# The S5 output factors move from two single buffers into the shared ring of six

## The chip, the cores and the metric

The kernel runs as one launch on one core of one Trainium2 chip. The metric is the device time of an execution in microseconds (us). Three executions were timed and one further execution was profiled. The engines are TensorE (PE, with its weight loads shown apart as PEld), VectorE (DVE), ScalarE (ACT), GpSimd (POOL) and SyncE (SP). SP does no arithmetic here: it issues every DMA of the program, in one order that is fixed when the program is built.

## The reference, cut to what matters

A single trunk layer works on 256 context tokens and 256 latent tokens of width 2048. One input projection feeds two mixers: RWKV-7 with 16 heads, and an S5 state space of 64 groups with 64 complex states each, in both directions. An output projection, a ConvGLU channel mixer and a final norm follow. The part that matters here is the S5 output:

```python
sr, si = _s5_scan(bu_re, bu_im, lam_re, lam_im, s0, d == 1)
...
s5_y.append(jnp.einsum('ghp,btgp->btgh', lp['s5_c_re'][d], sr)
            - jnp.einsum('ghp,btgp->btgh', lp['s5_c_im'][d], si))
```

The kernel cuts the scan into chunks of 8 tokens. For that it needs C times the powers 0 to 8 of lambda (a complex product, so a real and an imaginary part with two products each), and from these the 8-token Toeplitz matrices that carry inputs to outputs inside a chunk.

## The kernel before, in words

The program has four stretches. The first modulates the tokens. The second projects them: 256 KB weight tiles `raw` (line 210, two buffers) are split into a high and a low part on ACT (L213) and DVE (L214), and PE multiplies them (L430). Beside the projections run the preparation of the RWKV factors (`prepare`: L570 to L692), five blocks of the modulation, and two functions that turn S5 parameters into matrices: `s5_factors` (increments, L1319 to L1328, result `mbd` in DRAM) and then `s5_toeplitz` (outputs, L1181 to L1204, results `mcd` and `td` in DRAM). The third stretch is the recurrence: `chain` (L794 to L877) for RWKV and `s5` (L1337 to L1418). The channel mixer is the fourth.

`s5_toeplitz` works through 16 groups (two for each of the 8 passes of its outer loop), and a group has two blocks, the real and the imaginary part, so there are 32 blocks. For a group, SP loads 64 KB of C into a single buffer (L1170). For a block, DVE makes the first product `MCk` (L1181, 128x576) and POOL the second product `mck` (L1182); DVE combines them in `MCk` (L1184 for the real, L1187 for the imaginary part); four matmuls of PE read `MCk` (L1195), and SP stores it to `mcd` (L1199, 288 KB). After the second block ACT copies the bank out (`ks`, L1202, one buffer), SP stores it (`kd`, L1203), and after every second group SP copies `kd` to `td` in DRAM (L1204), which waits until both `kd` stores of the pass have landed.

Both `MCk` and `mck` have one buffer. So L1181 of a block waits until the store of the block before has landed, and L1182 waits until L1184 or L1187 of the block before has read `mck`.

Other work shares the queues there. POOL runs the forward substitutions of `solve` (L710 to L718: 31 steps of a product, L716, and a subtraction, L718). SP issues, when the projections have ended and their memory is free, a burst of loads for the scan: `U` (L1217), the first three `MB` (L1337) and `ul` (L1218). The loads of the chain come after the stores of the Toeplitz stage: `PT` (L794, L798) and `own` (L807). The chain's first matmuls are L831.

Pools are stacked. `pp`, the ring of six buffers, is closed when the RWKV preparation ends, and the space goes to `mw` (buffers of the later modulation's weights, `modw`, L374, 512 KB for each load), `yp` and the chain's pools. Every engine's order of instructions is set by a scheduler with a timeline of its own when the program is built; PE's order for L1195 is kept as written.

Of the kernel before, what the change touches and what calls it, by code (L numbers as in the profile page):

```python
# [10 lines left out]
F32 = mybir.dt.float32  # L11
# [144 lines left out]
class Body:  # L156
# [998 lines left out]
    def s5_toeplitz(self, pool):  # L1155


        nc, tc, V = self.nc, self.tc, self.nc.vector
        self.td = [tc.dram_tile([128, 8, 128], F32, name="td%d" % e) for e in range(8)]
        Bd = pool.tile([128, 4, 2, 2, 16], F32, name="s5Bd", bufs=1)  # L1160
        V.memset(Bd, 0.0)
        self.mcd = [tc.dram_tile([128, 2, 576], F32, name="mcd%d" % e) for e in range(16)]
        sh = [128, 4, 9, 16]
        for e in range(8):
            L, bb = self.s5_group(pool, e)
            kd = tc.dram_tile([128, 240], F32, name="kd%d" % e)
            for h in range(2):
                ee = 2 * e + h
                C = pool.tile([128, 4, 2, 16], F32, tag="C", name="C", bufs=1)
                nc.sync.dma_start(out=C, in_=self.A["s5c"][:, 2 * ee:2 * ee + 2].rearrange("p g d i h -> p (g d) i h"))  # L1170
                for par in range(2):
                    hr = slice(64 * par, 64 * par + 64)
                    nc.scalar.activation(out=Bd[hr, :, :, par], in_=bb[hr, 4 * h:4 * h + 4], func=AF.Copy)
                Lv = [L[:, :, i, 4 * h:4 * h + 4].rearrange("p t n -> p n t").unsqueeze(3).to_broadcast(sh)
                      for i in range(2)]
                Cv = [C[:, :, i].unsqueeze(2).to_broadcast(sh) for i in range(2)]
                ps = self.bank("d")
                for i in range(2):
                    MC = pool.tile(sh, F32, tag="MC", name="MCk", bufs=1)
                    t = pool.tile(sh, F32, tag="mt", name="mck", bufs=1)  # L1180
                    V.tensor_tensor(out=MC, in0=Cv[0], in1=Lv[i], op=ALU.mult)  # L1181
                    nc.gpsimd.tensor_tensor(out=t, in0=Cv[1], in1=Lv[1 - i], op=ALU.mult)  # L1182
                    if i == 0:
                        V.tensor_tensor(out=MC, in0=MC, in1=t, op=ALU.subtract)  # L1184
                    else:
                        fl = "p n t h -> p (n t h)"
                        V.scalar_tensor_tensor(out=MC.rearrange(fl), in0=MC.rearrange(fl), scalar=-1.0,  # L1187
                                               in1=t.rearrange(fl), op0=ALU.mult, op1=ALU.subtract)
                    with tc.manual_schedule(engines={mybir.EngineType.PE}):
                        for d in (1, 0):  # L1190
                            for g in range(2):
                                m = MC[:, 2 * g + d, 0:8]
                                m = m if d else m[:, ::-1]
                                o = 112 if d else 0
                                nc.tensor.matmul(ps[32 * g:32 * g + 32, o:o + 128],  # L1195
                                                 lhsT=Bd[:, 2 * g + d, i].rearrange("p a h -> p (a h)"), rhs=m,
                                                 start=(i == 0 and d == 1), stop=(i == 1 and d == 0),
                                                 skip_group_check=True)
                    nc.sync.dma_start(out=self.mcd[ee][:, i], in_=MC.rearrange("p n t h -> p (n t h)"))  # L1199
                    yield  # L1200
                ks = pool.tile([64, 240], F32, tag="ks", name="ks", bufs=1)
                nc.scalar.activation(out=ks, in_=ps[0:64, 0:240], func=AF.Copy)  # L1202
                nc.sync.dma_start(out=kd.rearrange("(h q) n -> q h n", q=8)[4 * h:4 * h + 4], in_=ks)  # L1203
            nc.sync.dma_start(out=self.td[e].rearrange("(s h) q n -> s (h q) n", s=8),  # L1204
                              in_=bass.AP(kd.tensor, kd.offset, [[16, 8], [240, 128], [1, 128]]))
# [165 lines left out]
    def s5_outputs(self, pool, half):  # L1371
# [4 lines left out]
        for e in range(8 * half, 8 * half + 8):  # L1376
            MC = pool.tile([128, 2, 4, 9, 16], F32, tag="MC", name="MC", bufs=3)
            nc.sync.dma_start(out=MC.rearrange("p i n t h -> p i (n t h)"), in_=self.mcd[e])
# [285 lines left out]
```

## Time and profile before

| what | value |
|---|---|
| median of three timed executions | 2175.01 us (2169.95 to 2193.74) |
| profiled execution | 2184.84 us, its span 2183.1 us |
| mean granted TensorE clock | 0.895 of full speed |
| PE busy | 1913.8 us (88%) |
| DVE busy | 1274.7 us (58%) |
| ACT busy | 897.1 us (41%) |
| POOL busy | 336.4 us (15%) |
| DMA | 433.80 MB, mean 199 GB/s |

The span runs from the first to the last instruction; 1.7 us of the execution lie outside it. Busy shares are averages over stretches with different limits. A time stamp in the rows below is counted from the start of the span.

### The profile page before, as it was taken

How to read it: one execution, taken by the hardware profiler on the slowest of the kernel's cores; microseconds unless marked ns; L12 is line 12 of the kernel's file. 1: busy time of each engine (PE TensorE's matmuls, PEld its weight loads, DVE VectorE, ACT ScalarE, POOL GpSimd, SP SyncE). 2: the span in 40 equal slices, each digit the busy share in tenths (PEclk: the TensorE clock that was granted, in tenths of full speed). 3: DMA queues.
4: the chain of work that ended last, by engine and by line, in shares of the span. 5: the costliest groups of instructions: out<-in, count | busy, mean ns of one | idle time of the engine just before them, and what ended most of it. 6: DMA issues, size and time to landing. Idle time of an engine off the chain costs nothing.

```text
span 2183.1 us, 35662 instructions
## 1 busy us (share of the span) xinstructions
PE 1913.8 (88%) x13704; PEld 1470.4 (67%) x13704; DVE 1274.7 (58%) x2400; ACT 897.1 (41%) x1617; POOL 336.4 (15%) x517
## 2 busy tenths in 40 slices
PE   4899998998989813369989999999999999999997
PEld 1557766666767712256655767788888888888886
DVE  7526766577878633276113587766666656655454
ACT  2234644444645502132113344454455545544442
POOL 0200043073183272252000100000000000000000
PEclk8899998999999855576678999999999999999998
DMA  8873566545445643476475785456666665566664
GB/s 322 307 265 97 170 221 227 184 138 181 140 137 176 207 171 113 145 247 227 155 232 196 270 316 181 155 193 220 224 222 215 217 231 178 190 180 185 187 186 141
DMA packets 181147, 433.80 MB, mean 199 GB/s; under 512 B 27248, under 2 KB 59376, under 8 KB 178160
## 3 DMA queue, kind: packets, MB, share of 16 engines
q1 hardware_dynamic: 180976, 431.52, 59.8%
q8 instruction: 108, 1.77, 0.3%
q14 instruction: 63, 0.52, 0.1%
HBM read 373.12 MB, written 62.52 MB: 200 GB/s over the span
## 4 chain that ended last, share of the span: by engine, by line
PE 58%; DMA 11%; DVE 9%; issue 2%; ACT 2%; POOL 2%; SPq 1%; DVEq 0%; ACTq 0%; POOLq 0%
PE ps_w L230 25%; PE ps_m L230 11%; PE ps_w L430 4%; DMA mcd<-MCk 3%; PE ps_d L379 3%; PE ps_c L841 2%; DMA raw<-wout_in 2%; PE ps_s L1404 1%; DMA MB<-mbd 1%; PE ps_s L230 1%; PE ps_g L663 1%; DMA kd<-ks 1%; DVE lo L214 1%; DMA modw<-modw_in 1%; DVE MCk L1181 1%
## 5 line engine op out<-in xcount | busy, mean ns | idle before, releaser
L220 DVE TENSOR_TENSOR lo<-raw,hi 128x1024 fp32r<-128x1024 f32 (+1 forms) x327 | 371.2, 1137 | 232.0 <-ACT hi L219 227.9
L219 ACT ACTIVATE hi<-raw 128x1024 fp32r<-128x1024 f32 (+1 forms) x327 | 322.6, 987 | 293.3 <-PE ps_w L230 202.4
L230 PE MATMUL ps_m<-h,hi 128*128 128x512 f32 x688 | 248.2, 399 | 2.0 <-ACT hi L219 2.0
L230 PE MATMUL ps_w<-h,hi 128*128 128x512 f32 x688 | 248.6, 400 | 0.8 <-DVE h L1516 0.8
L230 PE MATMUL ps_w<-hid,hi 128*128 128x512 f32 x704 | 247.6, 398 | 0.0
L230 PE MATMUL ps_w<-hid,lo 128*128 128x256 f32 x704 | 195.1, 281 | 0.0
L230 PE MATMUL ps_m<-h,lo 128*128 128x256 f32 x688 | 187.9, 283 | 1.1 <-DVE lo L220 1.1
L230 PE MATMUL ps_w<-h,lo 128*128 128x256 f32 x688 | 186.5, 281 | 0.3 <-DVE lo L220 0.3
L430 PE MATMUL ps_w<-hhi,lo 128*128 128x512 f32 (+2 forms) x448 | 173.1, 387 | 10.7 <-DVE lo L214 10.6
L430 PE MATMUL ps_w<-hhi,hi 128*128 128x512 f32 (+2 forms) x448 | 174.4, 389 | 8.4 <-ACT hi L213 8.4
L214 DVE TENSOR_TENSOR lo<-raw,hi 128x512 fp32r<-128x512 f32 (+1 forms) x144 | 110.7, 772 | 120.2 <-ACT hi L213 110.8
L430 PE MATMUL ps_w<-hlo,hi 128*128 128x512 f32 (+2 forms) x448 | 167.7, 374 | 0.0
L213 ACT ACTIVATE hi<-raw 128x512 fp32r<-128x512 f32 (+1 forms) x144 | 88.7, 619 | 170.0 <-DMA raw<-win_in 74.6
L230 PEld LDWEIGHTS ps_w<-h,hi 128*128 128x128 f32 x688 | 129.2, 188 | 41.2 <-ACT up L238 10.9
L230 PEld LDWEIGHTS ps_w<-hid,hi 128*128 128x128 f32 x704 | 131.3, 188 | 31.4
L230 PEld LDWEIGHTS ps_m<-h,hi 128*128 128x128 f32 x688 | 130.0, 189 | 30.2 <-ACT hi L219 2.8
L230 PEld LDWEIGHTS ps_m<-h,lo 128*128 128x128 f32 x688 | 130.6, 190 | 5.6 <-DVE lo L220 1.8
L230 PEld LDWEIGHTS ps_w<-hid,lo 128*128 128x128 f32 x704 | 133.0, 189 | 1.5
L230 PEld LDWEIGHTS ps_w<-h,lo 128*128 128x128 f32 x688 | 129.9, 189 | 3.6 <-DVE lo L220 0.7
L1195 PE MATMUL ps_d<-MCk,s5Bd 128*32 128x128 f32 x256 | 31.9, 394 | 107.9 <-DVE MCk L1187 70.6
L430 PEld LDWEIGHTS ps_w<-hhi,lo 128*128 128x128 f32 (+1 forms) x448 | 87.9, 196 | 45.6 <-DVE lo L214 21.9
L430 PEld LDWEIGHTS ps_w<-hhi,hi 128*128 128x128 f32 (+1 forms) x448 | 88.4, 197 | 37.4 <-ACT hi L213 15.6
(387 smaller groups left out, 3633.7 us busy)
## 6 DMA issues: line engine op xcount, KB each, us to landing
raw<-wup_in SPq DMA_DIRECT2D x176, 512.0 KB
modw<-modw_in SPq DMA_DIRECT2D x152, 512.0 KB
raw<-wdn_in SPq DMA_DIRECT2D x80, 512.0 KB
raw<-win_in SPq DMA_DIRECT2D x140, 256.0 KB
own<-own SPq DMA_DIRECT2D x32, 1024.0 KB
modw<-modw_in SPq DMA_DIRECT2D x80, 256.0 KB
own<-own SPq DMA_DIRECT2D x32, 640.0 KB
raw<-wout_in SPq DMA_DIRECT2D x38, 256.0 KB
```

The lines of the kernel that those rows point to most:

```text
L213: nc.scalar.activation(out=hi, in_=raw, func=AF.Copy)
L214: nc.vector.tensor_tensor(out=lo, in0=raw, in1=hi.bitcast(F32), op=ALU.subtract)
L219: nc.scalar.activation(out=hi, in_=src, func=AF.Copy)
L220: nc.vector.tensor_tensor(out=lo, in0=src, in1=hi.bitcast(F32), op=ALU.subtract)
L230: mm = self.nc.tensor.matmul(out, lhsT=a, rhs=b, start=(n == 0), stop=(n == last), skip_group_check=True)
L379: self.behind(nc.tensor.matmul(ps[32 * j:32 * j + 32, :], lhsT=self.silu[:, k], rhs=ws[j], start=(k < 4), stop=(k >= 12)))
L430: self.nc.tensor.matmul(out, lhsT=w[:, j], rhs=x[:, k, lo:T], start=(k == 4 * job["qs"][0] and n == 0), stop=(k == 4 * job["qs"][1] - 1 an ...
L663: mm = nc.tensor.matmul(pss[h][:, 128 * c:128 * c + w], lhsT=BK[hr, 4 * s + c], rhs=X[hr, c, x1:x1 + w], start=True, stop=True)
L841: nc.tensor.matmul(U[q:q + 64, i], lhsT=pt[q:q + 64, :, 8 * i + n], rhs=Ws[q:q + 64, i], start=True, stop=True)
L1181: V.tensor_tensor(out=MC, in0=Cv[0], in1=Lv[i], op=ALU.mult)
L1195: nc.tensor.matmul(ps[32 * g:32 * g + 32, o:o + 128], lhsT=Bd[:, 2 * g + d, i].rearrange("p a h -> p (a h)"), rhs=m, start=(i == 0 and d = ...
L1404: nc.tensor.matmul(outs[q], lhsT=X, rhs=m[:, ::-1] if d else m, start=False, stop=(d == 1 and i == 1))
```

## The change

The two tiles of a block no longer have one buffer each in the pool `tp`. They are taken from `pp`, whose six buffers were used until then by the early modulation and by `s5_factors`. Shapes, instructions and their number stay as they are. Two of the six buffers go to each block, so a buffer comes round again after three blocks. The first blocks follow the last tiles of `s5_factors` in that ring. `C`, `ks` and `s5Bd` keep one buffer each, and the bank `d` stays single.

```diff
@@ s5_toeplitz
                 ps = self.bank("d")
                 for i in range(2):
-                    MC = pool.tile(sh, F32, tag="MC", name="MCk", bufs=1)
-                    t = pool.tile(sh, F32, tag="mt", name="mck", bufs=1)
+                    MC, t = (self.pp.tile([128, 576], F32, tag="pp", name=name, bufs=6)
+                             .rearrange("p (n t h) -> p n t h", n=4, t=9) for name in ("MCk", "mck"))
                     V.tensor_tensor(out=MC, in0=Cv[0], in1=Lv[i], op=ALU.mult)
                     nc.gpsimd.tensor_tensor(out=t, in0=Cv[1], in1=Lv[1 - i], op=ALU.mult)
```

The scheduler lays out every engine anew for this. On PE, around the last matmuls of the input projection (L430 with 32x256), there stood before (L1195 counts four matmuls for a block; L732 and L743 belong to the second half of `solve`):

```order
L430 MATMUL ps_w<-hhi,lo 32x256
L1195 MATMUL ps_d<-MCk,s5Bd 32x128 x32
L732 MATMUL ps_m<-AU,L_6698 32x32 x32
L1195 MATMUL ps_d<-MCk,s5Bd 32x128 x4
L732 MATMUL ps_m<-AU,L_6698 32x32 x32
L1195 MATMUL ps_d<-MCk,s5Bd 32x128 x4
L743 MATMUL ps_m<-PT,FN 32x32 x32
L1195 MATMUL ps_d<-MCk,s5Bd 32x128 x4
L743 MATMUL ps_m<-PT,FN 32x32 x32
L1195 MATMUL ps_d<-MCk,s5Bd 32x128 x60
```

and there stands now:

```order
L430 MATMUL ps_w<-hhi,lo 32x256
L1195 MATMUL ps_d<-MCk,s5Bd 32x128 x72
L1345 MATMUL ps_s<-U_8125,MB 64x64 x32
L732 MATMUL ps_m<-AU,L_6698 32x32 x32
L1345 MATMUL ps_s<-U_8125,MB 64x64 x16
L732 MATMUL ps_m<-AU,L_6698 32x32 x32
```

Behind the last projection matmul there were 104 matmuls of L1195, which is 26 blocks; now there are 72, which is 18 blocks or 9 groups. Fourteen blocks instead of six stand between the projections.

On SP, where the first stores of the Toeplitz stage stand among the weight loads of the projection, there stood before:

```order
L1199 DMA mcd_4158<-MCk 128x576
L210 DMA raw<-win_in 128x512
L1328 DMA mbd_2534<-MB 128x512
L374 DMA modw<-modw_in 128x1024
L1228 DMA ud_7178<-u 128x8x64
L1231 DMA uld<-ul 128x256
L210 DMA raw<-win_in 128x512
L374 DMA modw<-modw_in 128x1024 x2
L1170 DMA C<-s5c_in 128x128
L210 DMA raw<-win_in 128x512
L1199 DMA mcd_4158<-MCk 128x576
L210 DMA raw<-win_in 128x512 x2
```

and there stands now:

```order
L1170 DMA C<-s5c_in 128x128
L1228 DMA ud_7178<-u 128x8x64
L1231 DMA uld<-ul 128x256
L1199 DMA mcd_4158<-MCk 128x576 x2
L210 DMA raw<-win_in 128x512
L1148 DMA Ls<-s5Led 128x144
L1170 DMA C<-s5c_in 128x128
L1199 DMA mcd_4159<-MCk 128x576
L210 DMA raw<-win_in 128x512
L1203 DMA kd_4178<-ks 4x16x240
L1199 DMA mcd_4159<-MCk 128x576
```

A weight load now follows one or two stores of `MCk`, where several weight loads followed one store before. The three loads of `modw` have left this place; two of them now stand just ahead of the last `td` copy and the chain's `PT` loads, and the third behind those.

On POOL, where the last `solve` begins (L710), the difference is this:

```order
 L1320 TENSOR_TENSOR mt<-bs,Ls 128x512 x5
-L1182 TENSOR_TENSOR mck<-C,Ls 128x576 x2
-L589 MEMSET sg 128x8
+L589 MEMSET sg 128x8
+L1182 TENSOR_TENSOR mck<-C,Ls 128x576 x8
+L589 MEMSET sg 128x8
+L1182 TENSOR_TENSOR mck<-C,Ls 128x576 x8
+L710 MEMSET TM 128x1024
 L1182 TENSOR_TENSOR mck<-C,Ls 128x576
-L589 MEMSET sg 128x8
-L1182 TENSOR_TENSOR mck<-C,Ls 128x576 x3
-L710 MEMSET TM 128x1024
```

Before, 6 of the 32 products of L1182 stood ahead of the last `solve`, 8 inside it and 18 behind it. Now 18 stand ahead of it and 14 inside it, in pairs: one pair after 7 instructions of `solve`, the next after 23 more, and the other five pairs with 3 to 6 between them.

## Rows read from the trace of the kernel before

**Rows 1.** Page, busy tenths of PE in 40 slices of 54.6 us

```profile
PE   4899998998989813369989999999999999999997
```

**Rows 2.** Busy time by stretch; the last three columns are clock, DMA share and GB/s

```profile
700.00:720.00 20.00, 20.00 (x106) 13.78 (x105) 15.63 (x25) 9.24 (x20) 2.97 (x5) 1.00 0.66 211
720.00:740.00 20.00, 16.85 (x133) 14.46 (x131) 14.89 (x28) 14.84 (x36) 2.75 (x2) 0.83 0.65 217
740.00:760.00 20.00, 19.72 (x348) 16.33 (x347) 9.37 (x17) 12.33 (x26) 7.54 (x12) 0.83 0.43 136
...
860.00:880.00 20.00, 4.22 (x32) 2.32 (x33) 6.61 (x8) 1.96 (x6) 4.77 (x5) 0.50 0.33 108
...
920.00:940.00 20.00, 13.87 (x231) 13.11 (x233) 1.82 (x4) 6.80 (x18) 0.00 (x0) 0.50 0.91 275
```

**Rows 3.** Waits from 690 to 990 us: total, times, longest

```profile
DVE MCk L1181 <- DMA mcd<-MCk: 94.0, 25, 13.7
POOL mck L1182 <- DMA C<-s5c_in: 84.0, 14, 14.5
...
POOL mck L1182 <- DVE MCk L1184: 30.8, 12, 9.3
```

**Rows 4.** Chain that ended last, 690 to 990 us: start, duration, what

```profile
712.62 6.58 DMA raw<-win_in
...
863.69 1.09 PE ps_d L1195 x8
...
868.52 5.58 DMA mcd<-MCk
...
875.87 2.10 DMA mcd<-MCk
...
879.90 2.07 DMA mcd<-MCk
...
883.77 1.09 PE ps_d L1195 x8
...
905.54 2.54 DMA kd<-ks
```

**Rows 5.** Timeline of one group: start, duration, engine, line, instruction, idle before

```profile
863.26 0.38 SPq L1170 DMA_DIRECT2D C<-s5c_in  x1
...
865.47 1.21 POOL L1182 TENSOR_TENSOR mck<-C,Ls 128x576 f32<-128x576 f32 x1 [4.38 <-DMA C<-s5c_in]
866.15 1.14 DVE L1181 TENSOR_TENSOR MCk<-C,Ls 128x576 f32<-128x576 f32 x1 [2.52 <-DMA mcd<-MCk]
867.40 0.76 DVE L1184 TENSOR_TENSOR MCk<-MCk,mck 128x576 f32<-128x576 f32 x1
...
882.09 0.76 DVE L1181 TENSOR_TENSOR MCk<-C,Ls 128x576 f32<-128x576 f32 x1 [2.22 <-DMA mcd<-MCk]
```

**Rows 6.** Timeline from 685 to 780 us, where the projections end

```profile
710.60 1.06 SPq L374 DMA_DIRECT2D modw<-modw_in  x2
...
759.44 0.28 PE L430 MATMUL ps_w<-hhi,lo 128*32 128x256 f32 x1
759.75 1.74 SPq L1217 DMA_DIRECT2D U<-ud  x4
...
767.46 0.81 SPq L1199 DMA_DIRECT2D mcd<-MCk  x1
...
776.44 1.04 DVE L1181 TENSOR_TENSOR MCk<-C,Ls 128x576 f32<-128x576 f32 x1 [13.66 <-DMA mcd<-MCk]
```

**Rows 7.** Groups of instructions from 690 to 990 us: the last `solve` on POOL

```profile
L718 POOL TENSOR_TENSOR TM<-TM,tmp 128x31 f32<-128x31 f32 (+15 forms) x31 | 19.8, 639 | 2.2
L716 POOL TENSOR_TENSOR tmp<-AU,TM 128x31 f32<-128x31 f32 (+15 forms) x31 | 18.4, 592 | 2.0
```

**Rows 8.** Timeline from 905 to 990 us, where the chain begins

```profile
909.04 1.46 SPq L794 DMA_DIRECT2D PT<-pt  x2
...
931.28 0.45 PE L831 MATMUL ps_c<-ZE,own 128*64 128x64 f32 x2 [2.04 <-ACT ZE L814]
```

## The prediction

> **What bounds the kernel now.** I read the busy slices first. PE fills nearly every slice of the page but one run of four in the middle, where it falls to 1 to 6 tenths [rows 1]. The windows say what kind of stretch that is: from 860 to 880 us PE works 4.22 of 20 us, DVE 6.61, POOL 4.77, the DMA engines are at a third, and the granted clock is 0.50, the level of 1.2 GHz [rows 2]. No engine is full, so it is a stretch of latency. The list of waits names what it waits for: DVE's L1181 stood 94.0 us behind the store of `MCk`, and POOL's L1182 stood 84.0 us behind the load of C and 30.8 us behind DVE's L1184 [rows 3]. The chain of waits gives the rhythm: from one `td` pass to the next it is 863.69 to 883.77, 20.08 us for two groups, 10.04 us a group, and in each pass 5.58 + 2.10 + 2.07 = 9.75 us of the chain are store waits of the kind that the single buffer makes [rows 4].
>
> The stretch that can shrink begins at the last projection matmul, which ends at 759.7, and it ends at the first `PT` load at 909.0 [rows 6, 8]. That is 149.3 us, and 26 of the 32 blocks lie in it. Everything behind it, the chain's first matmul at 931.28 to begin with [rows 8], hangs on loads that SP issues after the last `td` copy.
>
> **The change, part by part.** No instruction is added or removed. What goes is the wait for the landed store and the wait of L1182 for L1184. What is late next is a sum of terms.
>
> *Term 1, eight blocks move into the projections.* PE's order has 18 blocks behind the last projection matmul in place of 26. The eight cost PE 8 x 1.09 / 2 = 4.4 us [rows 4], against 3.4 us that PE is idle from 700 to 760 [rows 2]. They cost DVE 8 x (0.76 + 0.76) = 12.2 us [rows 5], against 20.1 us of DVE idle there [rows 2]. If that cover held, the projections would end as now, at 759.7. SP is why it may not hold: a weight load now stands right behind one or two stores of `MCk`, which wait for a group's whole computation, and the weight tile has only two buffers. Were each of the seven groups there to take the 10.04 us of the present rhythm, with as much again for the last weight tile, the projections would run from 700 to 780. The three `modw` loads leave this place, which helps: a weight load issued behind two of them took 6.58 us [rows 4, 6]. Neither bound is nearer; I take 10 us of delay, an end at 770, and keep 760 and 780.
>
> *Term 2, up to the last six groups.* Three of the nine groups left run beside the burst of `U`, `MB` and `ul` loads, which remains: from its first issue to the landing of the store behind it are 759.75 to 776.44, 16.7 us [rows 6]. Beside it POOL has a pair of L1182 and then 23 instructions of `solve`, at (19.8 + 18.4) / 62 + 0.07 = 0.69 us each [rows 7], so 15.9 us, plus the pair of 2.4 us [rows 5]: 18.3 us. The two overlap. I take 19 us, and keep 16.7 and 24 us (a group's time more, should they not).
>
> *Term 3, the rhythm of six groups.* C has still one buffer: a load is issued when both products of the group before are made and the real part's store has been issued. From a load's issue to L1182 are 2.21 us, then two L1181 beside POOL at 1.14 us each, then L1184 at 0.76 us [rows 5], and with the store's issue and the signals some 0.6 us more: 5.9 us. POOL on its side has two products of 1.21 us [rows 5] and 3 to 6 instructions of `solve` at 0.69 us: 5.4 us. I take 6 us, keep 5.4 us below and 7 us above (half of the 2.54 us of a `kd` landing [rows 4] added, as every second group's store stands behind a `td` copy). Five periods are 30 us. The last group then needs 2.4 us on POOL, 0.8 us on DVE, 1.09 us on PE, about 0.5 us on ACT, 2.54 us for `kd` and 0.7 us for `td` [rows 4, 5]: 8 us.
>
> *Term 4, the moved `modw` loads.* They are 3 x 512 KB, and they now compete with the loads of the chain, where DMA already stands at 0.91 and 275 GB/s [rows 2]. At that rate 1.5 MB take 5.7 us. I take 5 us; they cost nothing if the chain waits for something else.
>
> *Sum.* 770 + 19 + 30 + 8 + 5 = 832 in place of 909: a gain of 77 us. The profiled execution of 2184.84 us becomes 2107.8. It stands 9.8 us above the median shown; counted from the median it is 2098. I put the number between them, at 2103. The bounds: 759.7 + 16.7 + 27 + 8 = 811.4 is a gain of 98 us, 2077 from the median; 780 + 24 + 35 + 8 + 6 = 853 is a gain of 56 us, 2129 from the profiled execution.
>
> The rows speak against a part of the change at one point: a product L1181 takes 1.14 us beside an L1182 on POOL and 0.76 us without one, while L1182 has its 1.21 us either way [rows 5], and the change puts every pair of L1181 beside a pair of L1182. With the price of 0.76 us a period would be 0.7 us shorter and five of them 3.5 us, which gives 2104 in place of 2108. The Trainium skill (GPSIMD Engine Reference, section Specifications) has a rule for it: GpSimd's SBUF interfaces are shared with VectorE, and VectorE instructions with two SBUF inputs contend with it. By that rule the dearer price holds, and the trace agrees, with VectorE as the one that pays.
>
> **The rivals.**
> - *C's single buffer keeps the old rhythm.* Then the change does less than it says. For it: 84.0 us of POOL's waits are for C [rows 3]. Against it: C's load waited in turn for L1181 of the imaginary part, which waited for a store. The last six groups at 10.04 us would make 770 + 19 + 50 + 10 + 5 = 854, a gain of 55 us: 2130 from the profiled execution. Chance 0.10.
> - *The weight loads are held longer than I take.* Six blocks, three groups, fill the 60 us before 759.7 today, 20 us a group, since DVE, ACT and POOL have other work in order between them. At 15 us a group the projections end at 700 + 105 + 10 = 815, and the sum is 877: a gain of 32 us, 2153 from the profiled execution and 2143 from the median. Chance 0.12.
> - *The third stretch gives some back.* From the first `PT` load to the first L831 are 22.2 us today [rows 8]. If the moved loads and a less lucky order doubled that, the gain is 77 - 22 = 55 us, 2130. Chance 0.08.
> - *Slower: SP's order ties the projections to the Toeplitz stage at today's pace.* The place is the weight load behind the stores of `MCk`; the price is seven times a group's time. At 20 us a group the projections end at 850, the sum is 912, and nothing is gained. Each further us a group costs 7 us, so from 23 us a group it is slower by over 1%; at 25 us it gives 947, that is 2223. Against it: of those 20 us, store waits and the waits of L1182 for L1184 are a part that the change removes. Chance 0.03 for slower and 0.05 for the ground around zero.
>
> **How the numbers follow.** The forecast has 0.62, with a range of its own of 2077 to 2129. The two cases at 2130 lie beside it, and the held weight loads reach from there to 2153. A range of 2077 to 2146 takes in the forecast, both cases at 2130 and about half of the held loads; outside are the rest of these (0.06), the ground around zero and the slower case (0.08) and a gain over 98 us (0.04): 0.18. About 1%, 22 us, is what a measurement of this kernel can tell from no change. Faster by more than that are the forecast, the old rhythm, the held loads and the third stretch: 0.92. Within it 0.05, slower 0.03.
>
> **What would show it.** In the profile of the changed kernel the wait of L1181 for `MCk`'s store should be gone. The last L430 should end at 760 to 780; later than that, and waiting for weights behind stores, it is the held loads. Behind it there should be about 60 us to the first `PT` load, with L1182 waiting for C for some 2 us a group and POOL busy with `solve` in between. A period near 10 us in the last six groups would show C's buffer as the new wait. The first L831 should follow the first `PT` load by 22 to 28 us. A shift of the third stretch that is smaller than the shift of the `PT` load would make term 4 wrong.

## The result, and the profile after the change

| | before | changed |
|---|---|---|
| median of the runs | 2182.14 us (4 runs, 2169.95 to 2193.74) | 2099.99 us (4 runs, 2091.06 to 2104.55) |
| profiled execution, span | 2183.1 us | 2099.2 us |

The ratio is 0.9619, with a 95% interval from 0.955 to 0.9688. The forecast was 2103 us, with a range of 2077 to 2146.

The page of the changed kernel answers to [rows 1]. The hole in the middle of PE's slices is smaller, and it is no longer a run of four slices at 1 to 6 tenths. The second row, the clock that PE was granted, becomes important further down.

```profile
PE   3899998998998872659989999999999999999997
...
PEclk9999998999979975676988999999999999999999
```

The waits from 690 to 990 us answer to [rows 3] (total, times, longest). L1181's 94.0 us behind `MCk`'s store have no row any more. L1182's wait for C is down from 84.0 to 16.6 us, its wait for L1184 from 30.8 to 2.2 us. What is new is that DVE's L1181 now waits for C as well.

```profile
DVE MCk L1181 <- DMA C<-s5c_in: 27.6, 8, 11.2
POOL mck L1182 <- DMA C<-s5c_in: 16.6, 7, 4.5
...
POOL mck L1182 <- DVE MCk L1184: 2.2, 1, 2.2
```

The timeline of PE and SP answers to [rows 6, 8] (start, duration, engine, line, instruction). The three rows are the end of the projections, the first `PT` load, and the first matmul of the chain.

```profile
775.33 0.28 PE L430 MATMUL ps_w<-hhi,lo 128*32 128x256 f32 x1
...
848.95 2.49 SPq L794 DMA_DIRECT2D PT<-pt  x1
...
880.04 0.37 PE L831 MATMUL ps_c<-ZE,own 128*64 128x64 f32 x1
```

**Where the 83.9 us of span went.** The first `PT` load moved from 909.0 to 848.9, which is 60.1 us. From there to the first L831 it is 31.1 us in place of 22.3, a loss of 8.8. From the first L831 to the first load of the output projection (`wout`), which I call the end of the third stretch, it is 296.0 us (880.0 to 1176.0) in place of 325.9 (931.3 to 1257.2), a gain of 29.9. All that follows is 2.7 us shorter. 60.1 - 8.8 + 29.9 + 2.7 = 83.9. So over 20 us were gained in a place that the change does not touch, where I had forecast a small loss.

The timeline of POOL shows the last groups. Each row is a pair of L1182, one group (start, duration, and in brackets the idle time before it).

```profile
778.70 3.48 POOL L1182 TENSOR_TENSOR mck<-C,Ls 128x576 f32<-128x576 f32 x2 [1.31 <-DMA C<-s5c_in]
...
798.87 2.38 POOL L1182 TENSOR_TENSOR mck<-C,Ls 128x576 f32<-128x576 f32 x2
...
804.55 3.50 POOL L1182 TENSOR_TENSOR mck<-C,Ls 128x576 f32<-128x576 f32 x2 [0.27 <-DMA C<-s5c_in]
...
814.90 3.48 POOL L1182 TENSOR_TENSOR mck<-C,Ls 128x576 f32<-128x576 f32 x2 [1.71 <-DMA C<-s5c_in]
...
838.99 3.47 POOL L1182 TENSOR_TENSOR mck<-C,Ls 128x576 f32<-128x576 f32 x2 [2.17 <-issue]
```

From 798.87 to 838.99 are five periods, 40.1 us, 8.0 us each in place of the old 10.04. The second thing to see is the duration: the pair at 798.87, beside whose first half DVE was waiting, takes 2.38 us, and the others take up to 3.50 us.

### The profile page after: what moved, and what is told of

The parts are those of the page before. It is cut to its first block, busy times and chain, and to the rows that moved or that the text cites. A ratio compares the mean times of both kernels' runs of the same rounds, so it can differ in the third digit from the quotient of the medians.

```text
span 2099.2 us, 35645 instructions
## 1 busy us (share of the span) xinstructions
PE 1872.6 (89%) x13704; PEld 1455.9 (69%) x13704; DVE 1295.6 (62%) x2400; ACT 898.2 (43%) x1617; POOL 347.9 (17%) x517
## 4 chain that ended last, share of the span: by engine, by line
PE 58%; DVE 10%; DMA 8%; POOL 4%; issue 3%; ACT 1%; SPq 0%; DVEq 0%; POOLq 0%; ACTq 0%
PE ps_w L230 27%; PE ps_m L230 12%; PE ps_w L430 4%; PE ps_d L379 2%; PE ps_c L841 1%; POOL TM L718 1%; PE ps_g L663 1%; POOL tmp L716 1%; DMA raw<-wout_in 1%; DMA modw<-modw_in 1%; PE ps_s L230 1%; PE ps_s L1345 1%; PE ps_s L1404 1%; DMA bs<-s5bbd 1%; DMA C<-s5c_in 1%
## 5 line engine op out<-in xcount | busy, mean ns | idle before, releaser
L430 PE MATMUL ps_w<-hhi,lo 128*128 128x512 f32 (+2 forms) x448 | 173.5, 388 | 15.5 <-DVE lo L214 15.4
L430 PE MATMUL ps_w<-hhi,hi 128*128 128x512 f32 (+2 forms) x448 | 174.6, 390 | 4.7 <-ACT hi L213 4.7
L430 PE MATMUL ps_w<-hlo,hi 128*128 128x512 f32 (+2 forms) x448 | 168.1, 375 | 0.0
L213 ACT ACTIVATE hi<-raw 128x512 fp32r<-128x512 f32 (+1 forms) x144 | 88.7, 619 | 170.2 <-DMA raw<-win_in 65.7
L430 PEld LDWEIGHTS ps_w<-hhi,lo 128*128 128x128 f32 (+1 forms) x448 | 88.3, 197 | 50.0 <-DVE lo L214 26.2
L430 PEld LDWEIGHTS ps_w<-hhi,hi 128*128 128x128 f32 (+1 forms) x448 | 89.0, 199 | 31.7 <-ACT hi L213 11.5
L430 PEld LDWEIGHTS ps_w<-hlo,hi 128*128 128x128 f32 (+1 forms) x448 | 88.8, 198 | 15.7 <-issue 2.9
```

Source lines behind the costliest of these rows:

```text
L213: nc.scalar.activation(out=hi, in_=raw, func=AF.Copy)
L430: self.nc.tensor.matmul(out, lhsT=w[:, j], rhs=x[:, k, lo:T], start=(k == 4 * job["qs"][0] and n == 0), stop=(k == 4 * job["qs"][1] - 1 an ...
```

## The experiments

The theory was that the store wait of L1181 was nearly the whole price, and that the third stretch is shorter because its granted clock is higher. Open were two rivals on the first point (both single buffers weigh alike; C's buffer is the next wait) and three on the second: the shorter gap ahead of the stretch sets the clock, the order of the work in it does, or it is chance. "Gap" is from the last L430 to the first `PT` load; "third" from that load to the first `wout` load; both from one profiled execution. Time and ratio are of all runs.

| kernel | last L430 | first PT | gap | third | clock in it | median us | ratio to before (95%) |
|---|---|---|---|---|---|---|---|
| before | 759.4 | 909.0 | 149.6 | 348.2 | 0.74 | 2182.14 | |
| changed | 775.3 | 848.9 | 73.6 | 327.1 | 0.80 | 2099.99 | 0.9619 (0.955 to 0.9688) |
| e2_store | 771.0 | 874.5 | 103.5 | 355.8 | 0.76 | 2139.84 | 0.9828 (0.9759 to 0.9897) |
| e3_mck | 763.2 | 908.3 | 145.1 | 325.0 | 0.82 | 2155.69 | 0.9884 (0.9824 to 0.9945) |
| e4_c2 | 781.2 | 849.7 | 68.5 | 348.0 | 0.78 | 2115.87 | 0.9699 (0.9636 to 0.9763) |
| e6_warm | 767.6 | 852.0 | 84.4 | 333.7 | 0.78 | 2115.03 | 0.9685 (0.9614 to 0.9757) |
| r1_before | 758.8 | 906.1 | 147.3 | 347.8 | 0.75 | 2178.31, one run | |
| r2_after | 772.6 | 849.4 | 76.8 | 318.7 | 0.83 | 2098.14 | 0.9624 (0.9588 to 0.966) |
| e7_dve | 771.3 | 849.1 | 77.8 | 358.5 | 0.76 | 2124.17 | 0.973 (0.9699 to 0.9761) |
| e8_dve_c2 | 777.5 | 843.2 | 65.7 | 298.6 | 0.87 | 2069.18 | 0.9493 (0.9464 to 0.9522) |
| e9_weave_after | 770.5 | 848.3 | 77.8 | 315.6 | 0.82 | 2084.63 | 0.9567 (0.9525 to 0.9608) |
| b_weave_before | 760.5 | 910.1 | 149.6 | 320.2 | 0.84 | 2152.27 | 0.9875 (0.983 to 0.9919) |
| e10_weave_dve_c2 | 777.8 | 843.2 | 65.4 | 305.1 | 0.83 | 2071.96 | 0.95 (0.944 to 0.9559) |

### One buffer at a time: e2_store and e3_mck

```
# e2_store, on the kernel before
-MC = pool.tile(sh, F32, tag="MC", name="MCk", bufs=1)
+MC = pool.tile(sh, F32, tag="MC", name="MCk", bufs=2)
# e3_mck, on the kernel before
-t = pool.tile(sh, F32, tag="mt", name="mck", bufs=1)
+t = pool.tile(sh, F32, tag="mt", name="mck", bufs=2)
```

> The kernel before with a second buffer for `MCk` alone, in the stage's own pool; `mck` stays single and the six early modulation buffers are not touched, so the three `modw` loads keep their early place. Theory (the store wait of L1181 was nearly the whole price): L1181's wait for `MCk`'s store is gone, a group is C's 2.2 us, two L1182 of 1.2 us with an L1184 and an L1187 of 0.77 us between and behind them, and 0.6 us of signals, about 6.8 us; 20 blocks in place of 26 lie behind the last projection matmul; 2100 to 2118 us. Rival (both single buffers weigh alike): L1182's wait for L1184 grows, the period stays at 8.5 to 9.5 us, 2130 to 2150 us. On the third stretch (first L831 to the first load of the output projection, 325.9 us before, 296.0 us with the change): if the granted clock behind a shorter gap sets it, it is between these two, nearer the shorter; if the moved `modw` loads and their order set it, it stays at 320 to 330 us.

> The kernel before with a second buffer for `mck` alone; `MCk` stays single. Theory (the store wait was nearly the whole price): L1181 still waits for the store, some 90 us over the stretch, 25 of 26 blocks stay behind the last projection matmul, the period falls by at most 1 us from 10.0 us; 2165 to 2182 us. Rival (both weigh alike): 2130 to 2150 us.

By the first `PT` load, e2_store has gained 34.5 us, e3_mck 0.7, and both together (the change) 60.1. So the two buffers do not add up: the second one of `mck` is worth nothing while the store wait stands. What the change has beyond e2_store is worth some 25 us more. That is the second buffer of `mck`, but also a third one of each tile, since the ring holds three blocks, and the `modw` loads that moved; these were not tried apart. The waits say why the single buffers do not add up, of e2_store first:

```profile
POOL mck L1182 <- DVE MCk L1184: 30.3, 11, 7.1
```

and of e3_mck:

```profile
DVE MCk L1181 <- DMA mcd<-MCk: 82.6, 26, 13.0
```

In e2_store the wait of L1182 for L1184 is as long as before [rows 3], and eight periods from 793.06 to 864.18 us average 8.9 us, not the 6.8 expected. The median of 2139.84 lies in the rival's range, and "nearly the whole price" is wrong: lifting the store wait alone gives 34.5 of 60.1.

The total of e3_mck surprised: 0.9884 of before, some 25 us and between the ranges of both accounts, with almost nothing gained by the first `PT` load. In the profiled execution 23.2 us of its gain are in the third stretch, 325.0 us in place of 348.2. That spoke against the gap as the cause, since this gap is as long as ever. In e2_store, whose gap is 46 us shorter, the stretch is longer than before (from the first L831 it is 336.0 us, over both expectations).

### Is it chance? r1_before and r2_after

Both kernels unchanged, traced once more.

> The kernel before, unchanged, for a second trace of it. Theory (each kernel's order in the third stretch sets its granted clock there and with it the stretch's length): from the first PT load to the first load of the output projection again 342 to 354 us (348.2 in the first trace), PE busy 295 to 308 us at a mean clock of 0.72 to 0.76. Rival (the clock of that stretch falls by chance from execution to execution, and the differences between kernels there are luck): anywhere from 325 to 356 us, as likely as not more than 8 us from 348.

> The changed kernel, unchanged, for a second trace of it. Theory (the order sets the third stretch): from the first PT load to the first load of the output projection 321 to 333 us (327.1 in the first trace), PE busy 265 to 278 us at a clock of 0.79 to 0.82, and 2090 to 2106 us in all. Rival (chance): 325 to 356 us, as likely as not more than 8 us from 327.

One row of each trace shows the third stretch (stretch, its length, busy time of PE, PEld, DVE, ACT and POOL, then clock, DMA share and GB/s). Before, first and second trace:

```profile
909.00:1257.20 348.20, 301.64 (x3419) 207.83 (x3417) 146.11 (x440) 85.27 (x198) 61.37 (x144) 0.74 0.67 223
```

```profile
906.10:1253.90 347.80, 300.95 (x3414) 208.76 (x3415) 145.57 (x440) 85.53 (x199) 62.56 (x144) 0.75 0.67 223
```

The changed kernel, first and second trace:

```profile
848.90:1176.00 327.10, 271.34 (x3684) 199.39 (x3685) 151.75 (x442) 92.69 (x206) 60.39 (x144) 0.80 0.74 247
```

```profile
849.40:1168.10 318.70, 264.51 (x3690) 194.99 (x3686) 150.50 (x441) 92.97 (x207) 60.40 (x144) 0.83 0.76 253
```

The kernel before repeats its 348 us within 0.4, its PE busy time within 0.7 and its clock within 0.01. The changed kernel repeats less closely, 8.4 us apart and 0.03 in the clock, beyond what I had expected, but both traces lie 20 to 30 us below before. Chance alone is out. And the difference is the clock: PE issues no fewer matmuls, 3684 and 3690 against 3419 (256 of the added ones are L732 and L743 of `solve`, which stand there now), yet is busy 30 to 37 us less. Of the same 512 matmuls of L841, one takes 299 ns in the second trace of before and 286 in that of the change (they overlap; together they keep PE busy for 57.7 and 46.8 us); of those of L379 that lie in the stretch, 868 against 679.

### Gap or order? e6_warm, b_weave_before and e9_weave_after

e6_warm keeps PE at work in the gap:

```
 with tc.manual_schedule(engines={mybir.EngineType.PE}):
+    for _ in range(3 if ee >= 10 else 0):
+        nc.tensor.matmul(ps[0:32, 256:512], lhsT=Bd[:, 0, 0].rearrange("p a h -> p (a h)"),
+                         rhs=Bd.rearrange("p n i a h -> p (n i a h)"), start=True, stop=True,
+                         skip_group_check=True)
     for d in (1, 0):
```

> The changed kernel with three added matmuls of 32x256 ahead of each pass of L1195 in the last six groups, 36 in all; they write columns of the bank that nothing reads. Nothing else is added. Theory (the granted clock behind the gap follows PE's idleness in it, and the third stretch gained by the clock): PE's busy share from 800 to 840 us rises from a quarter to over a half, the granted clock there leaves 0.50, the third stretch's mean rises from 0.83 to 0.88 or more and it falls from 296.0 us to 280 to 290 us; against that 0 to 8 us in the gap itself, where PE's passes get longer; 2085 to 2100 us. Rival (the third stretch gained by its order, and the clock follows its own load alone): clock and length of the third stretch stay as they are within 4 us, 2098 to 2110 us.

From 820 to 840 us the changed kernel and then e6_warm read:

```profile
820.00:840.00 20.00, 5.33 (x42) 2.94 (x40) 11.93 (x11) 2.94 (x9) 16.14 (x17) 0.50 0.45 147
```

```profile
820.00:840.00 20.00, 11.36 (x80) 6.44 (x76) 11.41 (x9) 1.96 (x6) 16.85 (x21) 0.91 0.50 157
...
860.00:880.00 20.00, 15.90 (x244) 13.69 (x246) 0.86 (x2) 10.25 (x21) 0.00 (x0) 0.50 1.00 285
```

The clock in the gap rose from 0.50 to 0.91 with PE's busy time, and it was back at 0.50, the level of 1.2 GHz, 20 us later. The third stretch did not follow: its clock was 0.78, and from the first L831 it was 313.7 us long, more than either account expected, as is the median of 2115.03 us. The clock raised in the gap was not carried into the stretch behind it. The order of PE's work there was laid anew too, though (3622 matmuls lie in the stretch, against 3684), so this run alone does not set the gap aside. The gap was 8 to 11 us longer, since the projections ended 5 to 8 us earlier and the first `PT` load came 3 us later, so nothing was won.

The other two edits leave all that lies ahead of the third stretch alone, and change one number that interleaves its two parts. The traces agree: up to the first `PT` load PE has the same 5160 matmuls in the same order in b_weave_before as before, and the same 4904 in e9_weave_after as in the changed kernel.

```
-run(b.paced(woven(b.rwkv(first[0], lx, mx, pl), b.s5(sx, sb), 140, 100), late, 12))
+run(b.paced(woven(b.rwkv(first[0], lx, mx, pl), b.s5(sx, sb), 120, 100), late, 12))
```

> The same one number changed in the kernel before. Theory: the first PT load stays at 906 to 909 us; the stretch behind it, 348 us in both traces of the kernel before, changes by more than 8 us with the clock, to anywhere from 300 to 365 us, so 2130 to 2200 us. Rival: 344 to 352 us, 2170 to 2190 us.

> The changed kernel with one number changed: in the third stretch the two interleaved parts are taken 120 to 100 steps in place of 140 to 100, so that the order of the work changes there and nowhere before the first PT load. Theory (the order of that stretch decides its granted clock and length): the first PT load stays at 849 within 3 us, and the stretch from it to the first load of the output projection leaves the 319 to 327 us of the changed kernel by more than 10 us, longer or shorter, the mean granted clock moving the other way by 0.03 or more and the whole time with it: 2065 to 2090 us or 2110 to 2135 us. Rival (what lies ahead of the stretch, the shorter gap, decides its clock): 315 to 331 us there, 2090 to 2106 us in all.

On the kernel before the edit gained about 28 us, with the first `PT` load where it was within 1 to 4 us. The stretch of b_weave_before, and then the same 120 us of r1_before and of b_weave_before:

```profile
910.10:1230.30 320.20, 262.39 (x3455) 183.74 (x3452) 145.75 (x442) 84.57 (x200) 59.95 (x144) 0.84 0.77 255
```

```profile
1010.00:1130.00 120.00, 111.95 (x1019) 72.92 (x1018) 23.82 (x79) 16.11 (x41) 3.79 (x4) 0.68 0.58 185
```

```profile
1010.00:1130.00 120.00, 108.60 (x1285) 71.53 (x1284) 31.53 (x108) 20.73 (x56) 3.79 (x4) 0.87 0.76 236
```

PE is busy for nine tenths of the 120 us in both, but at a clock of 0.68 it gets through 1019 matmuls and at 0.87 through 1285 (of L1404, the most frequent, 322 and 452). So the order of the work in that stretch alone moves the kernel by as much as the change's unforeseen part. The length of the gap does not order the table: behind gaps of 74 to 78 us the third stretch lies between 315.6 and 358.5 us, behind gaps of 145 to 150 us between 320.2 and 348.2. With that against the gap, and the repeats against chance, the order is what is left for that part; the change's own order was not tried with the old gap, so for it this is argued and not shown. On the changed kernel the same edit did less: its third stretch of 315.6 us lies inside the rival's 315 to 331, while its median lies in the theory's range. That run by itself decides nothing. Which property of an order lets the clock rise was not found.

### What limits the new rhythm: e4_c2, e7_dve, e8_dve_c2

```
# e4_c2, on the changed kernel
-C = pool.tile([128, 4, 2, 16], F32, tag="C", name="C", bufs=1)
+C = pool.tile([128, 4, 2, 16], F32, tag="C", name="C", bufs=2)
# e7_dve, on the changed kernel
-nc.gpsimd.tensor_tensor(out=t, in0=Cv[1], in1=Lv[1 - i], op=ALU.mult)
+(V if ee >= 10 else nc.gpsimd).tensor_tensor(out=t, in0=Cv[1], in1=Lv[1 - i], op=ALU.mult)
# e8_dve_c2: both, and
-ks = pool.tile([64, 240], F32, tag="ks", name="ks", bufs=1)
+ks = pool.tile([64, 240], F32, tag="ks", name="ks", bufs=2)
```

> The changed kernel with a second buffer for C. Theory (C's load is what the shortened rhythm now waits for, 44 us of DVE's and POOL's waits): the period of the last groups falls from 8.0 us to 5.5 to 6.5 us, 16 blocks in place of 18 lie behind the last projection matmul, 2080 to 2092 us against 2100. Rival (POOL, with a pair of L1182 at 3.5 us and three to six instructions of `solve` a group, is the floor): the wait for C goes, the period stays at 7 to 8 us, 2093 to 2100 us.

> The changed kernel with `mck` of the last six groups computed on DVE instead of POOL. Theory (the pair of L1182, stretched from 2.4 to 3.5 us by its neighbour on DVE, and the wait behind `solve` on POOL make the 8.0 us of a group): four DVE products of 0.76 us, 3.1 us, behind C's load of 2.2 us and 0.6 us of signals, about 6 us a group, so 73.6 us from the last projection matmul to the first PT load become 60 to 66 us. Rival (the loads of C and the stores set the rhythm): 70 to 76 us. The whole time then hangs on the third stretch, whose order is laid anew as well: 2070 to 2110 us by the theory.

> As the run before it, with two buffers each for C and for `ks` as well. Theory: C's load then lies beside the products, a group is 3.1 us of DVE and signals, 4 to 5 us, unless `solve` on POOL or the load of the powers `Ls` ends later; 50 to 60 us from the last projection matmul, itself at 775 to 785, to the first PT load, which stands at 830 to 840. Rival (another load, that of `Ls`, is the next wait, as with two buffers of C alone): 65 to 70 us. The third stretch from the first PT load to the first load of the output projection 325 to 356 us, as in the other orders, so 2065 to 2110 us in all.

In e4_c2 the period fell to 6.1 us (six groups begin between 802.93 and 833.4), as the theory had it. But the projections end 5.9 us later, the first of these groups begins 4 us later, and from the last of them to the first `PT` load it is 16.3 us in place of 10.0, so that load does not move. With a third stretch of 348.0 us its median is some 16 us above that of the change, outside both ranges.

In e7_dve the gap did not shrink at all: 77.8 us, just over the rival's 70 to 76. POOL's pair was not the only thing in the way. The median of 2124.17 us missed the theory's range too, with the longest third stretch of all, 358.5 us. Its products on DVE show the contention, by their neighbour on POOL: at 811 us `solve` runs there, at 838 nothing does.

```profile
811.16 1.17 DVE L1182 TENSOR_TENSOR mck<-C,Ls 128x576 f32<-128x576 f32 x1
...
837.79 0.75 DVE L1182 TENSOR_TENSOR mck<-C,Ls 128x576 f32<-128x576 f32 x1
```

Both edits together, with `ks` doubled, give the fastest kernel of all: 2069.18 us, 0.9493 of before. Its gap of 65.7 us and its first `PT` load at 843.2 are the rival's, for L1181 waits 24.8 us, 17.2 of them at once, for the load of `Ls`. Its third stretch of 298.6 us is far under the 325 to 356 expected. Against the second trace of the change that is 6.2 us at the first `PT` load and 20.1 us in the third stretch, whose clock of 0.87 is the highest seen.

> The fastest kernel so far (`mck` of the last six groups on DVE, two buffers each for C and `ks`, on top of the change) with the same number changed. Theory: its third stretch is 298.6 us long at a granted clock of 0.87, the best of the orders seen; another order is likelier worse than better, 300 to 345 us, 2070 to 2115 us. Rival: 295 to 305 us and 2065 to 2078 us, because the gap of 66 us ahead of it decides.

With the interleaving at 120 to 100 on top, 2071.96 us: no difference that can be told, and both accounts allow it.

## Why the prediction was right, step by step

The total came within 4 us of the median by luck: two errors, of 22 and 29 us, cancelled in it. What held is the mechanism ahead of the first `PT` load: the wait of L1181 for the store is gone, and the projections end within their bounds. The rhythm behind them was mis-sized, and the gain of the third stretch was in no term.

- **Term 1, the projections' end.** Forecast 770, bounds 760 to 780; 775.6 and, in the second trace, 772.9. The direction and the bounds held. The cover on DVE was nearly used up: from 700 to 760 us it is busy 55.4 us (17.74 + 19.73 + 17.94 in the three windows) where it was 39.9 [rows 2], 15.5 more in place of the 12.2 I had counted, because products beside POOL's took longer than 0.76 us. On PE I counted half of the 1.09 us that a block took at a clock of 0.50 [rows 2, 4], 4.4 us for the eight. From 700 us to the last L430 the matmuls of L1195 keep it busy for 10.6 us, against 4.6 before: 6.0 us more.
- **Term 2, up to the last six groups.** Forecast 19, bounds 16.7 to 24; 23.3 us (775.6 to 798.87). The `solve` instructions took 16.8 us (782.1 to 798.9) for the 15.9 worked out. The pair ahead of them began 3 us after the last L430 and took 3.48 us, not 2.4.
- **Term 3, the rhythm.** Forecast 6 us, bounds 5.4 to 7; 8.0 us, outside. This is the step that was mis-sized, by 10 us over five periods. Three things lengthen it; what each is worth was not tried apart. First, the pair of L1182 takes about 3.5 us. Second, L1184, which stands between C's load and the real part's store, takes 1.75 or 1.76 us in five of the six groups, beside POOL's second product, and I had priced it at 0.76:

```profile
806.90 1.76 DVE L1184 TENSOR_TENSOR MCk<-MCk,mck 128x576 f32<-128x576 f32 x1
```

  Third, I took C's load to stand right behind the real part's store in SP's order. It does in three of the five periods, as at 802.33, but at 826.84 a load of factors stands between, and at 810.84 two such loads and the imaginary part's store, as SP's rows show:

```profile
801.89 0.33 SPq L1199 DMA_DIRECT2D mcd<-MCk  x1
802.33 0.36 SPq L1170 DMA_DIRECT2D C<-s5c_in  x1
...
808.69 0.32 SPq L1199 DMA_DIRECT2D mcd<-MCk  x1
809.07 0.42 SPq L1148 DMA_DIRECT2D Ls<-s5Led  x1
809.84 0.47 SPq L1199 DMA_DIRECT2D mcd<-MCk  x1
810.40 0.38 SPq L1152 DMA_DIRECT2D bs<-s5bbd  x1
810.84 0.70 SPq L1170 DMA_DIRECT2D C<-s5c_in  x1
```

  The pair at 804.55 follows the first load, and the pair at 814.90 the second, 10.35 us later. The second load was also slower: the pair began 4.1 us after its issue, against 2.2 us after that of the first.
- **The tail.** Forecast 8 us; 10.0 (838.99 to 848.95).
- **Contention.** I wrote that L1182 has its 1.21 us either way and that VectorE is the one that pays. Both pay. Over all their instances the median of L1182 went from 1212 to 1665 ns, that of L1181 from 759 to 982 and of L1184 from 758 to 913. Not every product pays: the second of the pair at 798.87 kept its 1.21 us beside an L1184 of 1.75 us. The Trainium skill (GPSIMD Engine Reference, section Specifications) says that the two engines share SBUF interfaces and contend when a VectorE instruction has two SBUF inputs; these rows agree and give it a size. The error came from reading one row in which only half of the product on POOL had a neighbour.
- **Term 4 and the third stretch.** Forecast a loss of 5 us. From the first `PT` load to the first L831 it is 31.1 and 29.3 us, outside the 22 to 28 that I gave, so a loss of 7 to 9 us is there. I did not separate it from the order of PE's work: PE has 320 instructions in those 31.1 us against 135 in the old 22.3. The rest of the stretch more than gave it back. That a re-laid order can change the granted clock behind it was in none of my terms; I had only a rival in which the third stretch loses.
- **The sum.** Without term 4, which lies behind it, the first `PT` load was forecast at 770 + 19 + 30 + 8 = 827, bounds 811 to 847. It came at 848.9, 22 us later than forecast and 2 us outside the bounds. Behind it I had a loss of 5 us, and 23.8 us were gained: 29 us the other way. What is left of the two is 7 us in the total, and that makes 2103 look exact.
- **The rivals.** The old rhythm of 10.04 us did not stay, the projections were not held to 815, and SP did not tie them to a slow group. C's buffer is a wait, as e4_c2 shows, but one of some 2 us a period.

## What to carry to other kernels

When a single buffer holds back a chain of two engines, cost its waits together: one removed alone may give half, or nothing. Price a product that will run beside another engine's by a row in which both run for their whole length, and read from the order behind which stores the next load is issued. And when an edit lets a scheduler lay out the rest of the program anew, expect the later stages to move by a per cent or more either way, and compare the granted clock stage by stage before a cause is looked for in the edit.

## What the runs showed of the hardware

In the kernel before, another order of the third stretch's work alone raised its granted clock from 0.75 to 0.84. With PE busy all of a 20 us window, it was granted 0.50, the level of 1.2 GHz, from 969 to 989 us of the changed kernel, and 0.97, nearly all of it at 2.4 GHz, right behind:

```profile
969.00:989.00 20.00, 20.00 (x134) 12.66 (x134) 4.72 (x13) 1.59 (x4) 0.00 (x0) 0.50 0.30 105
989.00:1009.00 20.00, 20.00 (x279) 15.31 (x278) 5.24 (x16) 4.39 (x11) 0.00 (x0) 0.97 0.68 248
```

The 134 matmuls of the first window and the 279 of the second fill 20.00 us each, and of the same kinds the second holds about twice as many (L841 14 and 32, L831 8 and 16): the busy time of PE alone does not tell at which of its levels it runs. Over thirteen traces the third stretch lay between 298.6 us at 0.87 and 358.5 us at 0.76.
